# Keys and values of both full branches as one Strassen block of seven products, with the sums of h formed earlier

## Chip, cores, metric

One core of one Trainium2 chip. The metric is the device time of one launch in microseconds (us), the median of several executions.

## What is computed

One layer of a decoder, 512 tokens by 2048 channels, fp32. The part that matters here is the input projection and what it feeds:

```python
h = rms_norm(x, norm_g[l])
proj = h @ w_in[l]
q, kv, g_logits, z_a, uv, z_b, merge_logits = jnp.split(proj, SPLIT_IDX, axis=-1)
k_c, v_c, k_s, v_s, k_w, v_w = [t.reshape(b, s, A_KV_GROUPS, HEAD_DIM)
                                for t in jnp.split(kv, 6, axis=-1)]
# compress(): hid = silu(blocks of 32 rows of k_c (v_c) plus positions, times w1), then times w2
o_a = nsa_attention(q, k_c, v_c, k_s, v_s, k_w, v_w, g_logits, ...) * jax.nn.silu(z_a)
```

Three branches of attention (compressed `_c`, selected `_s`, window `_w`) have keys and values of 256 columns each: 4 groups of 64. The 48 gate columns `g_logits` weigh the branches. The rest of the layer (gated MLP branch, merge, output projection, per-layer embedding, final norm) is not touched.

## The kernel before

Every fp32 product is made of three fp32r matmuls. A matrix is split into a high part (a cast on ACT, `high`, L158) and a low part (a subtraction on DVE, `low`, L164), and hi·hi, hi·lo and lo·hi are summed in PSUM. The activation h lies in SBUF in both parts (`act_h`, `act_l`); weights are streamed.

The products of h are jobs in a list, and a generator (`gemm`) issues them in order. `fill(n)` takes n units of it (a unit is three matmuls in a T job), `finish(name)` runs it to the end of a job. So the order on PE is written by hand: whatever the main program issues between two calls stands there in each engine's queue, and each engine runs its queue in order. Three kinds of job are met here:

- T: 128 columns of weights stationary, all 512 tokens moving: 16 k × 3 = 48 matmuls of 512 columns; the result lies transposed (columns on partitions). q0 to q7, z0 to z7, kc0 and kc1 (keys, compressed branch), vc0 and vc1 (its values), k00 to k11 (keys of the other two branches) are T jobs.
- N: 128 tokens stationary, up to 512 columns of weights moving; 16 k × 4 token tiles × 3 = 192 matmuls. vs and vw are N jobs of 256 and of 304 columns (the last 48 of vw are the gates).
- S: a block of 2·c columns and all tokens is done with seven products of quarter blocks in place of eight (Strassen in Winograd's form); the products are named by digits and their order is "15", "63", "7", "24". It needs sums of quarters of the weights (`sum_to`, on DVE) and four sums of quarters of h. Job u, much later, is the first of the S jobs that use the sums of h.

A job takes its weights in subs: 12 matmuls with one piece of hi and lo. `split_to` keeps the splits two subs ahead of PE. Loads are issued on SP (`load_next`), three raw buffers; streamed hi and lo have a few buffers each. At each sub `pop()` takes an item off `background` and off `slow` at set rates; `flush()` runs what was put off in `deferred`, such as the second half of a split.

The order is kc0 kc1 vc0 vc1 k00 k01 k10 k11 vs vw q0 q1 z0 and so on. Compression runs beside k: token rows in `tok`, `ps_hid` (L1186), a chain of small DVE and ACT operations (L1190 to L1208, a tanh in it), then `ps_kc` and `ps_vc` (L1211, L1215). The four sums of h are made in four chunks (`h_chunk`, L483, 12 DVE operations each) beside k, vs, vw and q, through `h_stage` tiles and DMAs into DRAM (L511).

## Time and profile before

| | |
|---|---|
| median of 3 executions | 1515.46 us (1515.12 to 1515.68) |
| profiled execution | 1515.4 us, of it span 1513.7 us |
| mean granted TensorE clock | 0.998 |
| PE busy | 1502.4 us (99%) |
| DVE, ACT, POOL busy | 1216.4, 857.5, 377.6 us |

The span is what the profile covers, from the first instruction to the last. Rows of matmuls give the latency of one; they overlap, so the time that one takes of PE is the distance from its start to the next one's. Names are those of tiles (buffer numbers left out), L-numbers are lines of the kernel before.

### The profile page before, as it was taken

To read this page: it belongs to the slowest core of one execution; us is meant where nothing else is said; L and a number is where in the kernel's file an instruction comes from. 1 tells how busy PE (TensorE), PEld (TensorE's weight loads), DVE (VectorE), ACT (ScalarE), POOL (GpSimd) and SP (SyncE) were. 2 spreads that over 40 slices of the span, in tenths; PEclk is the share of its full clock that TensorE was granted. 3 is DMA by queue.
4 is the path that set the end of the run, shared out by engine and by line. 5 is a ranking of instruction groups with operands and counts; after the bars stand their busy time and mean duration, and the time that the engine had idled before them with its cause. 6 is when DMAs were issued, how large, how long until landed. Compare 5 with 4: busy or idle time off the path is not lost.

```text
span 1513.7 us, 20632 instructions
## 1 busy us (share of the span) xinstructions
PE 1502.4 (99%) x7269; PEld 1261.9 (83%) x7269; DVE 1216.4 (80%) x1871; ACT 857.5 (57%) x1492; POOL 377.6 (25%) x595
## 2 busy tenths in 40 slices
PE   9999999999999999999999999999999999999997
PEld 8889988888888888888888888888888888888886
DVE  7557768899997888978888878797877985687877
ACT  6544456777675565555655555555556555444556
POOL 1311223323433232333333424421110002100000
PEclk9999999999999999999999999999999999999999
DMA  9676778778776895978686968896797869945555
GB/s 329 188 167 199 236 158 213 180 158 240 168 189 214 254 294 142 293 153 283 145 266 180 271 179 262 235 305 250 271 322 245 246 188 332 312 169 183 181 208 192
DMA packets 187351, 340.54 MB, mean 225 GB/s; under 512 B 12520, under 2 KB 84848, under 8 KB 184048
## 3 DMA queue, kind: packets, MB, share of 16 engines
q0 software_dynamic: 67216, 168.42, 40.6%
q1 hardware_dynamic: 119888, 170.55, 35.0%
q8 instruction: 57, 0.93, 0.2%
q14 instruction: 46, 0.38, 0.1%
q10 hardware_dynamic: 144, 0.26, 0.0%
HBM read 278.88 MB, written 109.58 MB: 257 GB/s over the span
## 4 chain that ended last, share of the span: by engine, by line
PE 95%; DVE 3%; ACT 1%; DMA 0%; issue 0%; DVEq 0%; ACTq 0%
PE ps_m L399 7%; PE ps_m L401 7%; PE ps_m L400 7%; PE ps_wo L400 3%; PE ps_wo L401 3%; PE ps_wo L399 3%; PE ps_t L1323 2%; PE ps_za L427 2%; PE ps_za L425 2%; PE ps_za L426 2%; PE ps_u L399 2%; PE ps_ub L400 2%; PE ps_u L400 2%; PE ps_ub L401 2%; PE ps_pg L401 2%; PE ps_pg L399 2%
## 5 line engine op out<-in xcount | busy, mean ns | idle before, releaser
L164 DVE TENSOR_TENSOR ls<-b,hs 128x1024 fp32r<-128x1024 f32 x218 | 266.4, 1223 | 108.4 <-ACT hs L158 107.2
L158 ACT CAST hs<-b 128x1024 fp32r<-128x1024 f32 x218 | 229.3, 1053 | 200.1 <-PE ps_m L401 46.0
L158 ACT CAST hs<-raw 128x1024 fp32r<-128x1024 f32 x114 | 120.0, 1055 | 116.9 <-issue 34.1
L164 DVE TENSOR_TENSOR ls<-raw,hs 128x1024 fp32r<-128x1024 f32 x114 | 139.3, 1222 | 39.5 <-ACT hs L158 39.3
L164 DVE TENSOR_TENSOR lo<-raw,hi 128x512 fp32r<-128x512 f32 (+1 forms) x152 | 100.6, 668 | 36.4 <-issue 9.9
L158 ACT CAST hi<-raw 128x512 fp32r<-128x512 f32 (+1 forms) x152 | 89.8, 601 | 60.5 <-PE ps_pg L440 10.8
L399 PE MATMUL ps_m<-hs,act_h 128*128 128x512 f32 x256 | 100.1, 391 | 0.0
L401 PE MATMUL ps_m<-hs,act_l 128*128 128x512 f32 x256 | 99.7, 389 | 0.0
L400 PE MATMUL ps_m<-ls,act_h 128*128 128x512 f32 x256 | 99.6, 389 | 0.0
L282 DVE TENSOR_TENSOR b<-raw,b 128x1024 f32<-128x1024 f32 x72 | 87.7, 1218 | 2.6 <-DMA raw<-in_w_in_dram 2.6
L282 DVE TENSOR_TENSOR b<-b,b 128x1024 f32<-128x1024 f32 x72 | 87.7, 1218 | 0.0
L158 ACT CAST pth<-ps_t 128x512 fp32r<-128x512 f32 (+1 forms) x88 | 47.7, 543 | 47.5 <-PE ps_t L1323 46.9
L1282 ACT ACTIVATE prob<-prob,st 128x512 f32<-128x512 f32 (+3 forms) x128 | 70.7, 556 | 4.3 <-DVE st L1273 3.9
L358 POOL COPY pad_r<-pad_r 128x1 f32<-128x1 f32 x42 | 32.1, 764 | 136.4 <-ACT pad_r L357 136.4
L164 DVE TENSOR_TENSOR ptl<-ps_t,pth 128x512 fp32r<-128x512 f32 (+1 forms) x88 | 55.7, 637 | 10.7 <-ACT pth L158 10.0
L1273 DVE CUSTOM_DVE_ANT_0 prob<-ps_s,b 128x512 f32<-128x512 f32 (+3 forms) x128 | 56.2, 486 | 2.5 <-PE ps_s L1264 2.1
L401 PEld LDWEIGHTS ps_m<-hs,act_l 128*128 128x128 f32 x256 | 48.0, 188 | 10.1
L400 PEld LDWEIGHTS ps_m<-ls,act_h 128*128 128x128 f32 x256 | 48.1, 188 | 9.9
L399 PEld LDWEIGHTS ps_m<-hs,act_h 128*128 128x128 f32 x256 | 48.1, 188 | 9.8
L425 PE MATMUL ps_za<-act_h,hi 128*128 128x512 f32 x128 | 53.5, 418 | 0.0
L1298 DVE TENSOR_SCALAR prob<-prob,st,gates 128x512 f32<-128x512 f32 (+3 forms) x128 | 51.5, 455 | 1.8
L425 PE MATMUL ps_q<-act_h,hi 128*128 128x512 f32 x128 | 52.0, 407 | 0.0
(705 smaller groups left out, 4557.4 us busy)
## 6 DMA issues: line engine op xcount, KB each, us to landing
raw<-in_w_in_dram SPq DMA_DIRECT2D x112, 512.0 KB, 5.2
b<-in_w_in_dram SPq DMA_DIRECT2D x56, 512.0 KB, 6.5
o<-in_w_out_dram POOLq DMA_DIRECT2D x48, 512.0 KB, 8.0
t<-in_w_up_b_dram POOLq DMA_DIRECT2D x24, 512.0 KB, 8.1
raw<-in_w_ple_gate_dram SPq DMA_DIRECT2D x24, 512.0 KB, 3.7
b<-o SPq DMA_DIRECT2D x18, 512.0 KB, 6.3
o<-o POOLq DMA_DIRECT2D x16, 512.0 KB, 5.1
act_l<-gate POOLq DMA_DIRECT2D x8, 1024.0 KB, 13.0
```

The costliest lines, as they stand in the source:

```text
L158: nc.scalar.copy(hi, src)
L164: nc.vector.tensor_tensor(out=lo, in0=src, in1=hi.bitcast(F32), op=ALU.subtract)
L282: nc.vector.tensor_tensor(out=b[o], in0=b[x], in1=b[y], op=ALU.subtract)
L358: nc.gpsimd.tensor_copy(steps[:, 16 + i:17 + i], steps[:, i:i + 1])
L399: nc.tensor.matmul(o, ah, wh, start=st, stop=False, skip_group_check=go)
L400: nc.tensor.matmul(o, ah, wl, start=False, stop=False, skip_group_check=go)
L401: nc.tensor.matmul(o, al, wh, start=False, stop=sp, skip_group_check=go)
L425: nc.tensor.matmul(ps, hi[:, j], ah, start=st, stop=False)
L426: nc.tensor.matmul(ps, hi[:, j], al, start=False, stop=False)
L1273: nc.vector.tensor_tensor_reduce(out=pt[:, j * n:j * n + n], in0=o[:, j], in1=b0[:, 512 - n:], scale=-SLOPE[h], scalar=3.0e38, op0=ALU.add ...
L1282: nc.scalar.activation(sl, sl, AF.Exp, bias=st[:, 0, j, hh:hh + 1], scale=-1.0, accum_out=st[:, 1, j, hh:hh + 1])
L1298: nc.vector.tensor_scalar(out=sl, in0=sl, scalar1=st[:, 1, j, hh:hh + 1], scalar2=gates[:, i, gate:gate + 1], op0=ALU.mult, op1=ALU.mult)
```

## The change

- The four k jobs, vs and vw become one S job `kv` of 1024 columns: K and V of the window branch and K and V of the selected branch, seven products of 48 matmuls of 512 columns. Products 1 and 5 are split in halves of 512 columns on the streamed hi and lo tiles (`narrow`), the others on wider tiles `hs` and `ls`; one quarter of the weights is read twice. K comes out with tokens on partitions, so `turn_k` transposes it on PE (16 transposes of 128×128, `ps_kt`), and DMAs on POOL copy half of the rows across partitions.
- vc0 and vc1 become an N job `vcg` of 304 columns: 256 of the compressed values and the 48 gates, by two DMAs per load. It stands between kc0 and kc1. ACT copies its rows out, and `turn_vc` transposes them back (8 transposes, `ps_vct`).
- The order is kc0 vcg kc1 q0 kv q1 z0 and on.
- The sums of h are needed by kv, so they are made from vcg on, at 0.7 items per sub instead of 0.5, in place (`ob_h`, `ob_l`, `vt`) for three of them. They are still stored to DRAM for job u. The fourth goes through streamed tiles `h_hi`, `h_lo` to DRAM, and is read back into `ob_h` before product 7.
- The splits of w1 (compression) are put into `background` ahead of the chunks of h, at vcg's first subs; they stood behind vc0.
- The mask `b0` is made at the start of attention, and no longer ahead of the compression.

```diff
-    def h_chunk(c, pool):
+    def h_chunk(c, temps, homes):
...
+        def put(p, src):
+            o = homes[p][:, k1]
+            parts_later(o[:, :, lo_t], o[:, :, hi_t], src, lambda: nc.gpsimd.dma_start(hsum_dram[p][:, k1], o))
+
+        def put_7(src):
+            o = [stream.tile([P, 2, 256], F32R, tag=tag, name="h_" + tag, bufs=n) for tag, n in (("hi", 4), ("lo", 3))]
+
+            def store():
+                for sl, part in zip((lo_t, hi_t), o):
+                    nc.gpsimd.dma_start(h3_dram[:, k1, sl], part)
+            parts_later(*o, src, store)
...
+    def final_kv(t, c, o, src):
+        if o is None:
+            if t == 2:
+                kv_rows["last"] = quad["pool"].tile([P, 2, S], F32, tag="hs", name="c21", bufs=3)
+            o = kv_rows["last"][:, t - 2]
+            nc.scalar.copy(o, src)
+        b = 0 if c else 1
+        kv_rows[b, t] = o
+        split(vt[:, b, t, :, 0:HD], vt[:, b, t, :, HD:], o[:, 256:].rearrange("p (g d) -> p g d", g=GROUPS), later=True)
+        if t == 3 or b and t == 1:
+            deferred.append(partial(turn_k, b, t // 2))
+            if not b:
+                later(partial(turn_k, b, 0))
+
+    def turn_k(b, hf):
+        ps = bank("o", "ps_kt")
+        for a in range(2):
+            for t in range(2):
+                nc.tensor.transpose(ps[:, (2 * a + t) * P:(2 * a + t + 1) * P],
+                                    kv_rows[b, 2 * hf + t][:, a * P:a * P + P], ident)
...
+            for o in (ob_h, ob_l):
+                for e in range(2):
+                    g = slice(kk(b, e), 8, 4)
+                    nc.gpsimd.dma_start(o[rows[1 - e], g, sl], o[rows[e], g, sl])
+        deferred.append(lows)
...
+    def evac_vcg(ps):
+        for t in range(TT):
+            nc.scalar.copy(vc_rows["t"][:, t], ps[t][:, :256])
+            nc.scalar.activation(gates[:, t], ps[t][:, 256:304], AF.Tanh, scale=0.5)
+            nc.vector.tensor_scalar(out=gates[:, t], in0=gates[:, t], scalar1=1.0, scalar2=0.5,
+                                    op0=ALU.add, op1=ALU.mult)
+
+    def turn_vc(a):
+        ps = bank("s", "ps_vct")
+        for t in range(TT):
+            nc.tensor.transpose(ps[:, t * P:t * P + P], vc_rows["t"][:, t, a * P:a * P + P], ident)
+        evac_c(1, a)(ps)
...
-    for a in range(2):
-        add_job(Job(f"vc{a}", "T", w_in, C_KV + 256 + 128 * a, 128, KT, h_act, evac_c(1, a)))
...
-    add_job(Job("vs", "N", w_in, C_KV + 768, 256, KT, h_act, evac_v(0), vs_b))
-    add_job(Job("vw", "N", w_in, C_KV + 1280, 304, KT, h_act, evac_v(1), vw_b))
+    kc_job(0)
+    add_job(Job("vcg", "N", w_in, ((slice(0, 256), C_KV + 256), (slice(256, 304), C_G)), 304, KT, h_act, evac_vcg,
+                ("o", "o", "t", "t")))
+    kc_job(1)
...
+    def evac_kv(p, ps):
+        quad_kv(p, ps)
+        if p == "5":
+            for c in range(4):
+                nc.gpsimd.dma_start(ob_h[:, 2 * c:2 * c + 2], h3_dram[:, 2 * c:2 * c + 2])
+
+    q_job(0)
+    add_job(Job("kv", "S", w_in, C_KV + 1024, 512, KT, lambda p, k, t: kv_act(p, k, t), evac_kv, ("s", "g", "t"),
+                c2=C_KV + 512, narrow="15"))
...
+        state["pops"] = 0.7
+        finish("vcg")
+        fill(2)
+        turn_vc(0)
+        fill(2)
+        turn_vc(1)
+        fill(1)
...
-    with tc.tile_pool(name="hsum", bufs=1) as hsum:
-        state["rate"] = 0
-        for c in range(4):
-            background.extend(h_chunk(c, hsum))
-        state["pops"] = 0.5
-        finish("q1")
...
+    finish("kv")
+    assert not background
+    fill(8)
...
+    ph_x.close()
+    finish("q1")
```

What the change moves in three queues, row by row. First ACT, at the end of the N job that holds the gates. Before, this job is vw: its rows are split straight into `vt`, each followed by a gate's tanh (L571), and q0's weights stand behind.

```order
L158 CAST hi<-raw 128x512 x2
L158 CAST vt<-ps_vw_1589 128x4x64
L571 ACTIVATE gates<-ps_vw_1589 128x48
L158 CAST vt<-ps_vw_1590 128x4x64
L571 ACTIVATE gates<-ps_vw_1590 128x48
L158 CAST vt<-ps_vw_1591 128x4x64
L571 ACTIVATE gates<-ps_vw_1591 128x48
L158 CAST vt<-ps_vw_1592 128x4x64
L571 ACTIVATE gates<-ps_vw_1592 128x48
L158 CAST hi<-raw 128x512 x4
```

Now ACT at the end of vcg; `ob_l` and `h_hi` are highs of chunk 1 of h, `o_584` a scratch tile that holds vc's rows and the temporaries of h.

```order
L158 CAST ob_l<-o_584 128x2x256
L158 CAST h_hi<-o_584 128x512
L615 COPY o_584<-ps_vcg_625 128x256
L616 ACT_TABLE_LOAD
L616 ACTIVATE gates<-ps_vcg_625 128x48
L615 COPY o_584<-ps_vcg_626 128x256
L616 ACTIVATE gates<-ps_vcg_626 128x48
L615 COPY o_584<-ps_vcg_627 128x256
L616 ACTIVATE gates<-ps_vcg_627 128x48
L615 COPY o_584<-ps_vcg_628 128x256
L616 ACTIVATE gates<-ps_vcg_628 128x48
L158 CAST hi<-raw 128x512
```

The table load, which stood ahead of the tanh of the compression (L1205), moved to the first tanh of the gates, and two highs of h stand directly ahead of the copies.

PE at the same place, from vcg's last matmul on (line numbers of the kernel after; `ps_vct` are the transposes of vc's rows). Before, PE has no transposes of results here: vc0 and vc1 are T jobs.

```order
L461 MATMUL ps_vcg_628<-hi,act_l_95 128x304
L446 MATMUL ps_kc_1003<-act_h_88,hi 128x512
L447 MATMUL ps_kc_1003<-act_l_89,hi 128x512
L448 MATMUL ps_kc_1003<-act_h_88,lo 128x512
L446 MATMUL ps_kc_1003<-act_h_88,hi 128x512
L447 MATMUL ps_kc_1003<-act_l_89,hi 128x512
L448 MATMUL ps_kc_1003<-act_h_88,lo 128x512
L623 MATMUL ps_vct<-ident,o_584 128x128 x4
L446 MATMUL ps_kc_1003<-act_h_88,hi 128x512
```

Two units of kc1 stand between the two; the transposes read what the four copies write.

DVE around the compression's chain. Before (L1199 to L1208), the weights of a k job are split ahead of it.

```order
L642 TENSOR_TENSOR tok<-ps_vc_805,tok 64x8x32 x4
L164 TENSOR_TENSOR lo<-raw,hi 128x512 x4
L1199 TENSOR_TENSOR o_580<-ps_hid_947,o_580 64x136
L1199 TENSOR_TENSOR o_580<-ps_hid_948,o_580 64x136
L1200 TENSOR_TENSOR o_580<-o_580 128x136
L1202 TENSOR_TENSOR hid_c<-o_580 128x1
L1203 SCALAR_TENSOR_TENSOR o_580<-o_580,hid_c 128x128
L1206 SCALAR_TENSOR_TENSOR o_580<-o_580 128x128
L1208 TENSOR_SCALAR o_580<-o_580 128x4x32 x4
L558 TENSOR_TENSOR ob_l<-ps_k_899,ob_h 64x512 x2
```

After (L1277 to L1286 are the same operations); L301 is a sum of weights for product 5, L504 are sums of h, `b_1052` is kv's quarter of weights.

```order
L301 TENSOR_TENSOR b_1052<-b_1052,raw 128x1024
L164 TENSOR_TENSOR lo<-raw,hi 128x512 x2
L504 TENSOR_TENSOR o_584<-act_h_94,o_584 128x512
L504 TENSOR_TENSOR o_584<-o_584,act_l_95 128x512
L164 TENSOR_TENSOR ob_l<-o_584,ob_l 128x2x256
L164 TENSOR_TENSOR h_lo<-o_584,h_hi 128x512
L164 TENSOR_TENSOR lo<-b_1052,hi 128x512 x2
L1277 TENSOR_TENSOR o_584<-ps_hid_1200,o_584 64x136
L1277 TENSOR_TENSOR o_584<-ps_hid_1201,o_584 64x136
L1278 TENSOR_TENSOR o_584<-o_584 128x136
L1280 TENSOR_TENSOR hid_c<-o_584 128x1
L1281 SCALAR_TENSOR_TENSOR o_584<-o_584,hid_c 128x128
```

The chain now stands behind kv's first lows, a sum of kv's weights and operations of chunk 2 of h.

PE at the end of kv (`ps_kt` are the transposes of K's rows, `c_1932` a row tile that ACT copies out of `ps_kv`):

```order
L420 MATMUL ps_kv_1313<-hs,act_h_94 128x512
L421 MATMUL ps_kv_1313<-ls,act_h_94 128x512
L422 MATMUL ps_kv_1313<-hs,act_l_95 128x512
L592 MATMUL ps_kt<-ident,c_1932 128x128 x4
L592 MATMUL ps_kt<-ident,keep_1491 128x128
...
L446 MATMUL ps_q_1950<-act_h_88,hi 128x512
```

Before, vw's last matmul is followed by q0's first at once:

```order
L438 MATMUL ps_vw_1592<-hi,act_h_94 128x304
L439 MATMUL ps_vw_1592<-lo,act_h_94 128x304
L440 MATMUL ps_vw_1592<-hi,act_l_95 128x304
L425 MATMUL ps_q_1935<-act_h_88,hi 128x512
L426 MATMUL ps_q_1935<-act_l_89,hi 128x512
```

So between the N or S job's end and the q job that follows, transposes of the last rows now stand.

## The prediction

> **What bounds the kernel now.** I read the page's totals first, then the chain, then the stretch that the change rewrites, cut into windows by job. On the page:

> ```profile
> span 1513.7 us, 20632 instructions
> PE 1502.4 (99%) x7269; PEld 1261.9 (83%) x7269; DVE 1216.4 (80%) x1871; ACT 857.5 (57%) x1492; POOL 377.6 (25%) x595
> PE 95%; DVE 3%; ACT 1%; DMA 0%; issue 0%; DVEq 0%; ACTq 0%
> ```

> TensorE is the bound: 99% busy, 95% of the chain. A microsecond of matmul removed is a microsecond gained, and a microsecond that PE waits is one lost. The windows, one row per stage (busy us and instructions of each engine), run from the end of kc0 to the start of z0; before them and behind them the two programs issue the same matmuls.

> ```profile
> 47.00:57.95 10.95, 10.95 (x50) 9.05 (x49) 4.37 (x8) 4.14 (x10) 8.29 (x19) 1.00 0.73 216
> 57.95:79.88 21.93, 21.93 (x98) 18.08 (x97) 12.36 (x28) 10.45 (x26) 5.55 (x12) 1.00 0.64 185
> 79.88:128.53 48.65, 48.65 (x235) 40.87 (x234) 30.94 (x56) 23.34 (x47) 7.14 (x11) 1.00 0.77 184
> 128.53:151.57 23.04, 23.04 (x194) 23.03 (x192) 17.28 (x29) 9.78 (x20) 2.66 (x5) 1.00 0.63 191
> 151.57:178.03 26.46, 26.46 (x194) 26.46 (x193) 22.80 (x42) 12.82 (x28) 4.26 (x8) 1.00 0.75 221
> 178.03:199.81 21.78, 21.78 (x98) 18.02 (x97) 8.67 (x17) 7.55 (x17) 6.22 (x16) 1.00 0.90 255
> ```

> The rows are kc1; vc0 and vc1; the four k jobs with the compression; vs; vw; q0 and q1. PE is full in all, at granted clock 1.00. A matmul's row lasts longer than its share (they are pipelined), so I count from start to start: 96 matmuls of 512 columns in q's 21.78 us are 0.227 us each, 192 of 256 columns in vs's 23.04 us 0.120, 192 of 304 in vw's 26.46 us 0.138. The k row holds 192×0.227 = 43.6 and 5.1 of compression. DVE has 6 to 18 us to spare in every long row but vw's, where 3.7 are left.

> **The gross gain.** Behind kc0 the new stretch holds vcg (192 matmuls of 304 columns, vw's form, 26.5), kc1 (11.0), q0 and q1 (21.8), compression (5.1), kv (7 products × 48 = 336 matmuls of 512 columns, 336×0.227 = 76.2), and 24 transposes of 128×128. For those the nearest rows are eight of the same shape, and the matmul behind them:

> ```profile
> 26.27 1.03 PE L1034 MATMUL ps_x<-ident,xt 128*128 128x128 f32 x8
> 27.06 0.47 PE L438 MATMUL ps_pl<-hi,ob_h 128*128 128x512 f32 x1
> ```

> Eight take 0.79, so 24 take 2.4. Together 26.5 + 11.0 + 21.8 + 5.1 + 76.2 + 2.4 = 143.0 against 152.8 before: 9.8 us less, if PE never waits. So the question is how much of 9.8 us comes back as waits. DVE must do the sums of h (four chunks of 12 operations), vc's lows and kv's lows and sums in less PE time, and several PE instructions now stand close behind results of ACT and DVE. The prices:

> ```profile
> L164 DVE TENSOR_TENSOR lo<-raw,hi 128x512 fp32r<-128x512 f32 x46 | 31.1, 689 | 21.2 <-issue 6.5 <-PE ps_k L427 4.9 <-PE ps_q L427 4.1
> L483 DVE TENSOR_TENSOR h<-h,act_l 128x512 f32<-128x512 f32 x8 | 5.5, 692 | 0.3
> L282 DVE TENSOR_TENSOR b<-raw,b 128x1024 f32<-128x1024 f32 x72 | 87.7, 1218 | 2.6 <-DMA raw<-in_w_in_dram 2.6
> 135.30 0.69 DVE L483 TENSOR_TENSOR h<-h_b,act_h 128x512 f32<-128x512 f32 x1
> 136.02 0.69 DVE L483 TENSOR_TENSOR h<-h,act_l 128x512 f32<-128x512 f32 x1
> 136.63 0.68 DVE L164 TENSOR_TENSOR lo<-raw,hi 128x512 fp32r<-128x512 f32 x1
> L158 ACT CAST hi<-raw 128x512 fp32r<-128x512 f32 x48 | 28.9, 621 | 27.6 <-PE ps_q L426 8.4 <-PE ps_k L426 6.0 <-PE ps_vc L426 4.9
> L158 ACT CAST vt<-ps_vw 128x256 fp32r<-128x256 f32 x4 | 1.5, 368 | 0.0
> L571 ACT ACTIVATE gates<-ps_vw 128x48 f32<-128x48 f32 x4 | 0.8, 210 | 2.0 <-DVE vt L164 2.0
> ```

> A DVE operation of 512 elements is listed at 0.69; the next one starts 0.72 later if it needs the result (135.30 to 136.02), 0.61 if not (136.02 to 136.63). A chunk of h is thus 12×0.61 to 12×0.69, 7.3 to 8.3.

> **The waits, in PE's order.**

> (a) Start of vcg. DVE's rows there:

> ```profile
> 48.91 1.73 DVE L642 TENSOR_TENSOR tok<-ps_kc,tok 64x256 fp32r<-64x256 f32 x4 [2.84 <-ACT tok L638]
> 50.68 1.29 DVE L164 TENSOR_TENSOR lo<-raw,hi 128x512 fp32r<-128x512 f32 x2
> 45.00 0.56 POOL L1129 IOTA b<- 128x512 f32 x1 [11.21 <-DVE act_l L166]
> 45.64 0.90 POOL L1130 TENSOR_SCALAR_AFFINE_SELECT b<-b 128x512 f32<-128x512 f32 x1
> 50.08 1.21 POOL L1156 DMA_DIRECT2D o<-in_cmp_w_k_dram  x1
> o<-in_cmp_w_k_dram POOLq DMA_DIRECT2D x1, 512.0 KB, 5.1
> ```

> kc0's four token lows hold DVE until 50.6. Before, the job there has subs of 12×0.227 = 2.7 us, so two subs of lead cover it; vcg's subs last 12×0.138 = 1.7, and the third comes due near 50.4 with its low still to run: 0.65 lost (0 to 0.7). Two subs later the low stands behind the first split of the compression's weights w1. That split stood behind vc0, long after its data; now it stands in vcg's second sub, on ACT and DVE both. Its DMA leaves POOL at 48.6 (50.08 less the two operations on b, 1.5, which move to the attention's start) and lands 5.1 later, at 53.7, while PE needs the fifth sub's low near 54.5 and the split's own two operations and the low come first: nothing if the landing holds, 2.5 if the queue of weight loads delays it. I take 0.5.

> (b) End of vcg. Only six matmuls of kc1 (1.4 us) stand between vcg's last one and the transposes of vc (ps_vct), which read ACT's copies of all four banks. Interleaved with these copies are the gates' tanh, and ahead of the first tanh the table load that now is in the compression's chain:

> ```profile
> 93.28 0.18 ACT L357 COPY pad_r<-eps_t 128x1 f32<-128x1 f32 x1
> 93.48 1.28 ACT L1205 ACT_TABLE_LOAD   x1
> 94.77 0.31 ACT L1205 ACTIVATE o<-o 128x128 f32<-128x128 f32 x1
> ```

> Four copies (4×0.37), three tanh (3×0.21) and the load (1.28) are 3.4 us of ACT before the last copy is there, so PE waits 3.4 − 1.4 = 2.0 at least. That needs ACT free at vcg's end. It isn't: the highs of chunk 1's second and third sum (ob_l, h_hi, 0.62 each) stand ahead and wait for DVE's two subtractions, which stand behind a low whose buffer is released by vcg's last sub. Low, subtractions and highs overlap into about 1.9 more. I take 3.9; upper end 4.3. DVE loses the same time, because the gates' scaling stands next in its queue and waits for the tanh.

> The row shows a load of 1.28 us, 0.02 behind the copy before it. [...]

> (c) Compression. Its DVE chain before:

> ```profile
> 91.18 0.69 DVE L164 TENSOR_TENSOR lo<-raw,hi 128x512 fp32r<-128x512 f32 x1 [4.91 <-PE ps_k L427]
> 91.90 0.29 DVE L1199 TENSOR_TENSOR o<-ps_hid,o 64x136 f32<-64x136 f32 x1
> ...
> 95.12 0.29 DVE L1206 SCALAR_TENSOR_TENSOR o<-o 128x128 f32<-128x128 f32 x1 [1.16 <-ACT o L1205]
> 95.44 0.63 DVE L1208 TENSOR_SCALAR o<-o 128x128 f32<-128x128 f32 x4
> 98.00 0.38 PE L1211 MATMUL ps_kc<-o 128*128 128x128 f32 x2
> ```

> From 91.90 to 96.07 it takes 4.2, or 2.9 without the table load. Before, PE has 6.1 us of k matmuls between the start of the chain and ps_kc, and no wait. Now two lows of kv's second sub stand directly ahead of the chain (the order of DVE shows it), and the second of them needs a buffer that kv's first sub frees as it ends. PE has then one unit of three matmuls (0.7) before ps_kc. So PE waits 0.69 + 2.9 − 0.7 = 2.9, and some 0.1 for signals: 3.0. Lower end 1.6 (the chain's operations, 2.3, without their waits, less the unit), upper 4.0 (with one more operation ahead). Directly behind it, kv's next bank is held by q0, whose two lows stand behind the chain: 0 to 1.0; I take 0.5.

> (d) kv's first two products. Eight subs are 8×2.7 = 21.8 us of PE. DVE owes in them sixteen lows, four sums of weights, the last chunk of h, the chain and q0's lows: 16×0.61 + 4×1.22 + 7.8 + 2.9 + 1.4 = 26.7. With the 3.0 of (c) there is 24.8 of room, so 1.9 would be late if DVE had no lead; the last sub of product 5 also needs the last chunk's sums written. With the h temporaries' waits I reach 3.2 as the upper end; 0 if DVE enters with a lead of two subs. I take 1.6, and 0.3 (0 to 1.0) for the same backlog in kc1 and q0.

> (e) End of kv. PE's order has the transposes of the last K rows (ps_kt) directly behind kv's last matmul; they wait for two ACT operations of 512 columns (2×0.62) less what overlaps: 1.0 (0.6 to 1.2). Before, vw's banks were read by ACT while q0's matmuls ran.

> At nothing: kv's narrow DMAs and the h sums written to and read from DRAM, because each issue costs POOL half a microsecond and a sum is needed again no sooner than one product (10.9 us) later:

> ```profile
> 128.56 0.53 POOL L511 DMA_DIRECT2D hsum<-h_stage  x1 [8.18 <-DVE h_stage L164]
> raw<-in_w_in_dram SPq DMA_DIRECT2D x112, 512.0 KB, 5.2
> ```

> The weight loads on SP (5.2 to land) have three buffers, and kv takes five quarters of weights in 76 us. If that cover fails, a late load costs at most its landing, 5.2. The DMAs that copy K rows across partitions, and b's two operations, have q1 and z0 (14.8 us) before the first compressed scores: 8×0.53 + 1.5 + a landing of 5.2 is 10.9, so 0 to 1.0.

> **Sum.** Waits: 0.65 + 0.5 + 3.9 + 3.0 + 0.5 + 1.6 + 0.3 + 1.0 = 11.45. With all lower ends 2.0 + 1.6 + 0.6 = 4.2, with all upper ends 0.7 + 2.5 + 4.3 + 4.0 + 1.0 + 3.2 + 1.0 + 1.2 + 1.0 = 18.9. Net −9.8 + 11.45 = +1.65. The profiled execution took 1515.4 us (span 1513.7), within 0.1 of the median 1515.46, so 1517.1. The ends are 1515.4 − 5.6 = 1509.8 and 1515.4 + 9.1 = 1524.5.

> **Rivals.**
> 1. DVE becomes the bound (slower). From vcg to the end of product 5 PE has 26.5 + 11.0 + 10.9 + 5.1 + 0.8 + 21.8 = 76.1 us of own work. DVE has 16 lows of 304 columns (0.47), 76 operations of 512 elements (48 of h, 24 lows, 4 of w1; 0.69), 16 token lows (0.42), four sums (1.22), and 6.5 of chain, positions, gates and q0's lows: 7.5 + 52.4 + 6.7 + 4.9 + 6.5 = 78.0. My forecast grants it 76.1 + 10.45 (all waits but (e)) = 86.5, so it decides from 8.5 us of idle time of DVE on; each further one is one on the end. Its idle in the gates is 3.9. The row of lows above shows 21.2 us of idle ahead of 46, 0.46 each; 24 of them would add 11.0, if all of it were waits for buffers: 78.0 + 3.9 + 11.0 = 92.9, 6.4 over. With half of them it is 0.9 over. The middle, 3.6, gives 1520.7. For it speaks that two of my large waits are such buffers already; against it that before, DVE idled there because it was ahead.
> 2. DVE and ACT run ahead (faster). If chunk 1's highs are done when vcg ends, (b) is 2.0; if the lows come early enough, (c) is 1.6, (d) and (a) vanish and (e) is 0.6 to 1.0. Waits of 4.6: 1510.2. For it speaks the spare DVE time in the k and q rows; against it that buffers, not DVE's speed, hold the low in (b) and in (c).
> 3. A gap slows PE afterwards. (b) and (c) are waits of 3 to 4 us of a PE that had none in the rows above; if behind each the granted clock (1.00 in all six) stood at half for as long as the gap, matmuls would lose half of 3.9 + 3.0: 1517.1 + 3.4 = 1520.5. No row shows such a fall. [...] No gap of this trace can test it.

> **How the numbers follow.** 0.2% (3 us) is about what a measurement of this kernel can tell from no change. My forecast is that the waits eat the gain: 1517.1, own range 1512.4 to 1518.5, chance 0.38. Rival 1 has 0.28 and rival 3 0.06: slower 0.34. Rival 2 has 0.28: faster. Cases of both signs hold most of the chance, so the range goes out to the bounds of the sum: from 1509.0 (0.8 below the lower bound, which keeps (b) and (c) in any case) to 1522.5 (2.0 short of the upper one, which needs every wait at its worst; about 1 in 10 is left out at either end).

> **What would show it.** Right: vw's, vs's and vc's stages gone, kv 76 us of matmuls at 0.227; PE idle 2 to 4 us before the first ps_vct, released by ACT's copy; 2 to 4 before ps_kc, released by DVE's scaling; 1 before the last ps_kt, released by ACT. Wrong: PE's busy time in the stretch not 143 but more; less than 4 us of idle on PE; a wait for a DMA in kv; a granted clock under 1.00 behind a gap.

## The result and the profile after

The changed kernel takes 1535.78 us (median of 4, 1533.57 to 1538.05) against 1515.29: ratio 1.0135, 95% interval 1.0118 to 1.0153. It is 20.5 us slower. I had forecast 1517.1 with a range to 1522.5, so the forecast was wrong.

The profile's page has these lines where before's had PE at 99% and a clock of 9 tenths throughout (the third line is the granted clock in 40 slices of 38 us):

```profile
span 1535.4 us, 20496 instructions
PE 1505.3 (98%) x7149; PEld 1255.2 (82%) x7149; DVE 1247.4 (81%) x1897; ACT 870.7 (57%) x1509; POOL 390.2 (25%) x620
PEclk9979999999999999999999999999999999999999
```

Fewer matmuls are issued (7149 against 7269), and one slice, 77 to 115 us, has a mean clock of 0.7. The same stretch as in the prediction, from vcg's first matmul to z0, by windows (vcg; kc1; q0 with the hidden products; kv with the end of the compression; last transposes and q1; the column ahead of the last two is the granted clock, the next the share of the DMA engines):

```profile
47.17:75.52 28.35, 26.99 (x193) 26.49 (x192) 19.58 (x38) 13.43 (x37) 17.65 (x33) 1.00 0.87 258
75.52:97.13 21.61, 15.39 (x59) 11.70 (x58) 13.18 (x32) 10.17 (x26) 6.97 (x10) 0.76 1.15 277
97.13:118.31 21.18, 17.58 (x82) 14.51 (x81) 13.60 (x22) 8.42 (x21) 5.35 (x11) 0.84 0.99 305
118.31:206.95 88.64, 82.84 (x356) 65.85 (x354) 72.76 (x97) 42.97 (x67) 15.12 (x25) 0.98 0.71 193
206.95:219.63 12.68, 12.09 (x57) 9.97 (x58) 7.58 (x16) 7.12 (x17) 8.61 (x17) 1.00 0.73 169
```

Together 172.5 us where before had 152.8, so 19.7 of the 21.7 us between the two spans are lost here (the profiled execution took 1537.06 us, 1.3 above the median). kc1 takes 21.6 for 11 us of matmuls. The waits of PE (line, releaser: total us, times, longest):

```profile
PE ps_vct L623 <- issue: 4.9, 1, 4.9
PE ps_q L448 <- DVE lo L164: 3.6, 1, 3.6
PE ps_kc L1289 <- issue: 2.5, 1, 2.5
PE ps_kv L421 <- DVE lo L164: 2.0, 2, 1.3
PE ps_vcg L460 <- DVE lo L164: 1.4, 2, 0.8
PE ps_vct L623 <- ACT o L615: 1.3, 1, 1.3
PE ps_kv L420 <- DVE b L166: 1.0, 1, 1.0
PE ps_m L421 <- DVE ls L164: 1.0, 2, 0.7
PE ps_kt L592 <- ACT c L579: 0.6, 1, 0.6
```

These are the places that I had named, (a) to (e), and one that I had at 0.3: q0, 3.6. What stands ahead of the two longest is seen on ACT and DVE (start, duration, idle time ahead and its releaser):

```profile
79.76 0.62 ACT L158 CAST hi<-raw 128x512 fp32r<-128x512 f32 x1 [2.27 <-DMA h_d<-h_hi]
98.84 0.62 ACT L158 CAST hi<-raw 128x512 fp32r<-128x512 f32 x1 [3.40 <-DMA h_d<-h_hi]
100.61 0.69 DVE L164 TENSOR_TENSOR lo<-raw,hi 128x512 fp32r<-128x512 f32 x1 [4.23 <-DMA h_d<-h_lo]
```

A split of weights waits for a DMA that *stores* a sum of h, because the sum sits in a slot of the same ring of buffers. Ahead of ps_vct stands such a split in ACT's queue, then two highs of h and the copies; the store's 2.27 us are thus a part of PE's 4.93. And the matmuls behind the wait:

```profile
76.68 0.40 PE L448 MATMUL ps_kc<-act_h,lo 128*128 128x512 f32 x1
82.00 0.45 PE L623 MATMUL ps_vct<-ident,o 128*128 128x128 f32 x1 [4.93 <-issue]
83.74 1.24 PE L623 MATMUL ps_vct<-ident,o 128*128 128x128 f32 x3 [1.29 <-ACT o L615]
84.63 0.77 PE L446 MATMUL ps_kc<-act_h,hi 128*128 128x512 f32 x1
85.20 0.63 PE L447 MATMUL ps_kc<-act_l,hi 128*128 128x512 f32 x1
85.63 0.63 PE L448 MATMUL ps_kc<-act_h,lo 128*128 128x512 f32 x1
```

From 84.63 on a matmul lasts 0.63 in place of 0.39, and the next starts after 0.43 in place of 0.23: half clock (the granted clock reads 0.50 from 80 to 88 us).

### The profile page after: what moved, and what is told of

Read it like the earlier page. It is cut to its first block, busy times and chain, and to the rows that moved or that the text cites. A ratio compares the mean times of both kernels' runs of the same rounds, so it can differ in the third digit from the quotient of the medians.

```text
span 1535.4 us, 20496 instructions
## 1 busy us (share of the span) xinstructions
PE 1505.3 (98%) x7149; PEld 1255.2 (82%) x7149; DVE 1247.4 (81%) x1897; ACT 870.7 (57%) x1509; POOL 390.2 (25%) x620
## 5 line engine op out<-in xcount | busy, mean ns | idle before, releaser
L164 DVE TENSOR_TENSOR ls<-b,hs 128x1024 fp32r<-128x1024 f32 x224 | 273.9, 1223 | 110.7 <-ACT hs L158 109.1
L158 ACT CAST hs<-b 128x1024 fp32r<-128x1024 f32 x224 | 235.3, 1052 | 208.6 <-PE ps_m L422 51.0
L158 ACT CAST hs<-raw 128x1024 fp32r<-128x1024 f32 x126 | 132.8, 1054 | 122.5 <-issue 28.8
L164 DVE TENSOR_TENSOR ls<-raw,hs 128x1024 fp32r<-128x1024 f32 x126 | 154.1, 1223 | 41.1 <-ACT hs L158 40.8
L164 DVE TENSOR_TENSOR lo<-raw,hi 128x512 fp32r<-128x512 f32 (+1 forms) x128 | 83.8, 662 | 26.4 <-ACT hi L158 8.7
L158 ACT CAST hi<-raw 128x512 fp32r<-128x512 f32 (+1 forms) x128 | 74.8, 597 | 47.2 <-PE ps_pg L461 10.4
L301 DVE TENSOR_TENSOR b<-raw,b 128x1024 f32<-128x1024 f32 x78 | 95.1, 1219 | 4.9 <-DMA raw<-in_w_in_dram 4.8
L301 DVE TENSOR_TENSOR b<-b,b 128x1024 f32<-128x1024 f32 x72 | 87.8, 1219 | 0.0
L158 ACT CAST pth<-ps_t 128x512 fp32r<-128x512 f32 (+1 forms) x88 | 47.7, 544 | 48.1 <-PE ps_t L1405 47.5
L164 DVE TENSOR_TENSOR ptl<-ps_t,pth 128x512 fp32r<-128x512 f32 (+1 forms) x88 | 55.6, 636 | 10.2 <-ACT pth L158 9.5
L448 PE MATMUL ps_q<-act_h,lo 128*128 128x512 f32 x128 | 51.4, 402 | 3.6 <-DVE lo L164 3.6
## 6 DMA issues: line engine op xcount, KB each, us to landing
raw<-in_w_in_dram SPq DMA_DIRECT2D x112, 512.0 KB, 5.5
b<-in_w_in_dram SPq DMA_DIRECT2D x59, 512.0 KB, 6.7
o<-in_w_out_dram POOLq DMA_DIRECT2D x48, 512.0 KB, 8.3
t<-in_w_up_b_dram POOLq DMA_DIRECT2D x24, 512.0 KB, 8.5
raw<-in_w_ple_gate_dram SPq DMA_DIRECT2D x24, 512.0 KB, 3.8
b<-o SPq DMA_DIRECT2D x18, 512.0 KB, 6.2
o<-o POOLq DMA_DIRECT2D x16, 512.0 KB, 5.2
```

What stands on the lines that cost most here:

```text
L158: nc.scalar.copy(hi, src)
L164: nc.vector.tensor_tensor(out=lo, in0=src, in1=hi.bitcast(F32), op=ALU.subtract)
L301: nc.vector.tensor_tensor(out=b[o], in0=b[x], in1=b[y], op=ALU.subtract)
L448: nc.tensor.matmul(ps, lo[:, j], ah, start=False, stop=sp)
```

## The experiments

Every kernel is timed against the kernel before on the same chip. Unless said otherwise an edit is made to the kernel after. I had two new theories beside my forecast's waits: **the crowd** (DMAs are slow in this stretch and hold ring slots and weights back) and **the clock** (behind a wait PE runs at half clock for a while).

**1. No crowd.** The background loads (adding DMAs for sums of other weights, `t<-in_w_up_b`, 512 KB each) are issued at 0.7 per sub. vcg's subs last 1.7 us and not 2.7, so the unchanged rate per sub is a higher rate per microsecond (from 60 to 75.5 us five are issued, where before had two), and the stores of h come in the same stretch. First they were held back into kv, then behind kv:

```diff
-        state.update(rate=0.7, step=0)
+        state.update(rate=0.0, step=0)
...
-    state["rate"] = 0        # first kernel only, with rate 0 again behind kv
+    state["rate"] = 0.65
...
-    state.update(rate=1.2, step=None)   # second kernel only
+    state.update(rate=1.5, step=None)
```

> The kernel after, with the background loads (adding DMAs for sums of other weights, 512 KB each, on POOL's queue, 0.7 per sub) held back until the compression is done, and issued at 0.65 per sub during kv. Theory of the crowded queue (vcg's subs last 1.7 us in place of 2.7, so the same rate per sub puts these DMAs closer, and the stores of h land after 10 us in place of 4): the stores land in about 5 us, the waits ahead of ps_vct and in q0 shrink as without the ring, about 8 us less, near 1528, unless kv's own weight loads are delayed. Rival (the stores are slow by themselves): landings of about 10 us stay, 1536.

> The kernel after, with none of the background loads (512 KB adding DMAs on POOL's queue) from vcg to the end of kv; they come later, at 1.5 per sub in place of 1.2. Theory of the crowded queue: as with the loads held back to kv (the wait ahead of ps_vct 2.3, none of weight in q0), but without the 2.4 us wait for a weight load that they made in kv: the stretch from vcg to z0 some 5 us shorter than there, near 1528. What is left then are my forecast's waits for ACT and DVE: about 4.5 at ps_vct, 4 at ps_kc, 2.5 in kv's first products, 0.8 at its end. Rival (the wait in kv has its own cause): 1532 again.

Measured 1533.60 (ratio 1.0118, 1.0102 to 1.0133) and 1528.09 (1.0084, 1.0067 to 1.0101). The DMAs issued from 70 to 104 us, first after, then the first kernel (KB each, median us from issue to landing):

```profile
h_d<-h_hi POOLq DMA_DIRECT2D x2, 256.0 KB, 10.2
raw<-in_w_in_dram SPq DMA_DIRECT2D x4, 512.0 KB, 11.9
```

```profile
raw<-in_w_in_dram SPq DMA_DIRECT2D x5, 512.0 KB, 4.3
h_d<-h_hi POOLq DMA_DIRECT2D x2, 256.0 KB, 3.6
```

The landings fall to a third, as the theory has it. In the first kernel kv then waits for its own weights (2.4 us at one low); in the second nothing of that is left, and PE's waits are

```profile
PE ps_kc L1289 <- issue: 2.6, 1, 2.6
PE ps_vct L623 <- issue: 2.1, 1, 2.1
PE ps_kv L421 <- DVE lo L164: 2.0, 2, 1.3
PE ps_vct L623 <- ACT o L615: 1.4, 1, 1.4
```

with none at q0. The crowd costs 7.7 us (1535.8 to 1528.1), and what stays is my forecast's list and two spells of half clock.

**2. Own slots for h_hi and h_lo**, the crowd left in:

```diff
-            o = [stream.tile([P, 2, 256], F32R, tag=tag, name="h_" + tag, bufs=n) for tag, n in (("hi", 4), ("lo", 3))]
+            o = [cmp.tile([P, 2, 256], F32R, tag="h_" + tag, name="h_" + tag, bufs=1) for tag in ("hi", "lo")]   # chunks 0 to 2
```

> The kernel after, with h_hi and h_lo of the first three chunks on tiles of their own in place of slots of the streamed hi and lo rings. Theory of the ring (a slot that holds a sum of h is free only when its store into DRAM has landed, 10 to 11 us later, and the weights' splits queue behind it on ACT and DVE): the wait ahead of ps_vct falls from 5.1 to about 3 us, the 3.8 us wait in q0 goes, and with it q0's stretch at half clock (2.5): about 8 us less, near 1528. Rival (those splits are late because ACT's and DVE's queues are full): the same two waits, 1536.

Measured 1530.64 (1.0098, 1.0083 to 1.0114). The wait in q0 is gone, but ps_vct's grew from 4.9 to 6.8:

```profile
81.62 0.62 ACT L158 CAST hi<-raw 128x512 fp32r<-128x512 f32 x1 [4.49 <-DMA raw<-in_w_in_dram]
```

The same split now waits for its weights, which land after 15.2 us. So the slot is one way in which the crowded queues reach PE, and the late loads another; expectation right for q0, wrong for ps_vct.

**3. The table load ahead of vcg.**

```diff
         state["pops"] = 0.7
+        nc.scalar.activation(warm, eps_t, AF.Tanh)
         finish("vcg")
```

> The kernel after, with a tanh of one column ahead of vcg's last subs' evacuation, at vcg's start, so that the table load is done there. My forecast's step (the load of 1.28 us stands between the copies that ps_vct needs): the second wait at ps_vct (1.3 to 1.6 us, between its first transpose and the others) goes; 1.3 us less, 2 if the half clock ends sooner: 1534. Rival (the load is covered): 1536, or 1 more for the token lows that it delays at vcg's start.

Measured 1537.11 (1.0140, 1.0125 to 1.0155): no gain. The second wait at ps_vct went as expected, but q0's wait for the same DMAs rose from 3.6 to 5.4 us. What was gained ahead of the late DMA was lost again in the wait for it.

**4. Spare matmuls in the waits**, to keep PE busy.

```diff
+        for _ in range(20):     # ahead of ps_vct; 16 ahead of q0, 8 ahead of ps_kc
+            nc.tensor.matmul(ps, act_h(0, slice(0, P)), act_h(0), start=True, stop=True)
```

> The kernel after, with idle PE time filled: 20 spare matmuls of 512 columns ahead of the first ps_vct, 16 ahead of q0's first matmul and 8 ahead of ps_kc, each into a bank that the next real matmul starts afresh. Nothing else moves, and 44 matmuls (10 us of PE) are added. Theory of the clock (a PE that waits some 3 us falls to half clock and stays there for 5 to 8 us): the granted clock stays at 1.00 from 75 to 110 us, the matmuls of kc1 and q0 come every 0.227 us, about 8 us less, near 1528. Rival (the clock's fall costs nothing of its own; the waits for ACT, DVE and DMA set the time): 1536, or up to 2 more where the spare matmuls run over.

Measured 1536.21 (1.0132, 1.0115 to 1.0149): the same as after, so the forecast of 8 us failed. In q0, where the spares filled the wait, the clock stayed at 1.00 and z0 began 2.8 us earlier than in after (216.9 against 219.6). At ps_vct they ran out 1.6 us before the first copy was there, and the clock fell all the same, only later. Some 1.8 us of that were lost again behind z0, 1.0 of them in a wait for lows of weights in job vn that after doesn't have; why there, was not tried. As a test of the clock this one is inconclusive, so the clock was measured by itself.

**5. One wait in the kernel before**, between vs and vw, which nothing else depends on:

```diff
+        nc.tensor.transpose(gb[:, :P], hold, ident)
+        for _ in range(12):     # 30 in the other
+            nc.gpsimd.memset(hold, 0.0)
+        nc.tensor.transpose(gb[:, P:2 * P], hold, ident)
         finish("q1")
```

> The kernel before, with one wait put into PE's queue between vs and vw: a transpose, twelve small fills on POOL of the tile that it read, and a second transpose that needs the last fill. Nothing else depends on it, so the time is the wait plus what the clock adds. The wait is estimated at about 2 us. Theory of the clock (it falls only behind a wait of more than some 3 us): granted clock stays 1.00, +2 us, 1517.5. Rival (any wait of 2 us already halves it): 1520.

> As the kernel before with one wait between vs and vw, but of thirty fills, estimated at about 5 us. Theory of the clock: the granted clock falls to 0.5 in the wait and stays there for some 4 to 7 us of matmuls behind it; the time grows by the wait and 2 to 3.5 us more: 1522.5 to 1524. Rival (the clock's fall is a reading of the profile and costs nothing): the wait alone, 1520.4.

Measured 1521.59 (+6.1; ratio 1.0041, 1.0026 to 1.0056) and 1525.37 (+9.8; 1.0066, 1.0051 to 1.0081). The waits came out longer than estimated, 3.4 and 8.1 us from start to start:

```profile
151.38 0.27 PE L1228 MATMUL ps_gap<-ident,hold 128*128 128x128 f32 x1
154.86 0.48 PE L1231 MATMUL ps_gap<-ident,hold 128*128 128x128 f32 x1 [3.21 <-POOL hold L1230]
```

```profile
150.96 0.27 PE L1228 MATMUL ps_gap<-ident,hold 128*128 128x128 f32 x1
159.17 0.47 PE L1231 MATMUL ps_gap<-ident,hold 128*128 128x128 f32 x1 [7.94 <-POOL hold L1230]
```

The windows where the clock falls and where it returns, the short wait first:

```profile
152.00:154.00 2.00, 0.00 (x0) 0.00 (x0) 0.80 (x3) 0.30 (x1) 1.60 (x8) 0.93 0.00 0
160.00:162.00 2.00, 2.00 (x14) 2.00 (x14) 0.99 (x3) 1.07 (x2) 0.00 (x0) 0.87 0.49 148
```

```profile
154.00:156.00 2.00, 0.00 (x0) 0.00 (x0) 0.00 (x0) 0.00 (x0) 1.56 (x8) 0.82 0.00 0
162.00:164.00 2.00, 2.00 (x16) 2.00 (x16) 1.52 (x3) 0.45 (x1) 0.00 (x0) 0.97 0.02 3
```

A window of 2 us with a mean of 0.93 holds 0.28 us at half clock, so the short wait's half clock runs from 153.72 to 160.52, the long one's (0.82, 0.97) from 155.28 to 162.12: 6.8 us both times. Of the first, 5.7 fall on matmuls, which lose half of it: 3.4 + 2.8 = 6.2, measured 6.1. Of the second, 2.9 do: 8.1 + 1.5 = 9.6, measured 9.8. The clock costs time of its own (for the long wait the times alone don't show it, since the interval, 7.7 to 12.3 us, includes 8.1; for the short one they do), and a longer wait may pay less for it, since more of the spell passes in the wait. My expectation that the cost grows with the wait was wrong; as the short wait came out at 3.4 us, whether one of 2 us is free was not tested here. The fall came 2.2 us after PE's last matmul in one and 4.2 in the other, so not at a fixed time behind it.

**6. The transposes of vc later**, with no crowd and the table early:

```diff
-        fill(2)
+        fill(8)
         turn_vc(0)
```

> As the kernel without the crowd, and the tanh table loaded at vcg's start and eight units of kc1 (in place of two) ahead of the first ps_vct. Theory of the place (the transposes stand too close behind ACT's copies): the waits at ps_vct (4.5 in all) and the half clock behind them (1.2) go, 1.5 of them come back as a wait for the token lows ahead of ps_hid or in q0: near 1523. Rival (ACT and DVE owe the work anyway, and the wait moves on to kc1's weights): no more than 2 us less.

Measured 1523.40 (1.0054, 1.0039 to 1.0069). No wait at ps_vct is left, nor a fall of the clock there; 1.4 us came back as a wait for a low in q0 and 0.4 as one in kc1. The two edits were not tried apart, but the last of the four copies and the first transposes tell their shares:

```profile
79.49 0.43 ACT L615 COPY o<-ps_vcg 128x256 f32<-128x256 f32 x1
80.68 0.60 PE L623 MATMUL ps_vct<-ident,o 128*128 128x128 f32 x4
```

The copies are done 0.8 us before PE gets there. With the load of 1.28 us still between them they would have come some 0.5 us late (an estimate), so nearly all of the 4.7 us is the later place.

**7. Own slots again, and the last transposes of K a sub later**, on top of that kernel (for K: `deferred.append(lambda: deferred.append(partial(turn_k, b, t // 2)))`).

> The last kernel (no crowd, table early, transposes of vc eight units later) with h_hi and h_lo of the first three chunks on tiles of their own, and the last transposes of K deferred by one sub. Theory (the wait ahead of ps_kc is for a slot of the streamed lo ring that h_lo holds; the last ps_kt stands too close to its copies): ps_kc's wait 2.7 goes to about 1.3, half of the clock's fall behind it goes, the last wait at ps_kt 0.8 goes: near 1520. Rival (DVE's total work in the stretch is what binds, so what goes there returns in kv): 1523 as before.

Measured 1522.53 (1.0045, 1.0030 to 1.0060), 0.9 below experiment 6 and not clear of it: the intervals overlap. ps_kc's wait fell from 2.6 to 1.2 as expected. But the clock fell there nevertheless, and the wait at ps_kt stayed at 0.6, since only the other half of these transposes moved. The fall came at 109.72, about half way through a second wait of 1.0, so a wait of 1.2, ten short products and some 0.5 us more were enough for the clock.

**8. Ten spare matmuls ahead of that ps_kc**, the clock's second test:

```diff
         b = bank("o", "ps_kc")
+        for _ in range(10):
+            nc.tensor.matmul(b, act_h(0, slice(0, P)), act_h(0), start=True, stop=True)
```

> The kernel with own slots for h_hi and h_lo (no crowd, table early, transposes of vc later), with ten spare matmuls of 512 columns (2.3 us of PE) ahead of ps_kc, where PE waits 1.3 us and, right behind ps_vc, 1.3 again. Theory of the clock: the fall to half clock from 110 to 117 us, which I put at about 2.5 us there, doesn't come, and though work is added the time falls by 1.5 to 3 us: 1520. Rival (the clock's fall is not what costs there; PE waits for DVE's lows anyway): 1522.5 as before, or up to 1 more.

The windows of the kernel without the spares, then with them:

```profile
110.00:112.00 2.00, 1.63 (x4) 1.37 (x5) 1.97 (x4) 0.00 (x0) 0.00 (x0) 0.50 0.71 262
112.00:114.00 2.00, 2.00 (x6) 1.52 (x6) 1.89 (x4) 0.62 (x1) 0.00 (x0) 0.50 0.16 28
```

```profile
110.00:112.00 2.00, 1.79 (x8) 1.51 (x9) 1.97 (x4) 0.57 (x1) 0.00 (x0) 1.00 0.74 270
112.00:114.00 2.00, 2.00 (x11) 1.64 (x10) 2.00 (x4) 0.94 (x3) 0.00 (x0) 1.00 0.13 18
```

Eleven matmuls fit where six did. 2.3 us of work were added, the stretch from vcg to z0 is 2.3 us shorter (155.2 against 157.5), and the median is 1521.01 (1.0043, 1.0029 to 1.0057). That is 1.5 below, but single runs of the two kernels overlap and their ratios to before (1.0043 and 1.0045) are alike, so the trace shows it and the times only point to it.

**9. Additions of h on POOL, and a new order**, on top of experiment 7:

```diff
-                add(w[n], act_h(k1, t), act_l(k1, t))
+                nc.gpsimd.tensor_tensor(out=w[n], in0=x, in1=y, op=ALU.add)
```

> As that one, with the two first additions of each chunk of h on POOL in place of DVE (8 operations, some 5 us of DVE; an addition of this shape is 1.1 us on POOL in the trace of before). Theory of DVE as the bound in this stretch: the waits for lows in q0 (1.5) and in kv's first products (2.8) shrink by about 3 together: near 1517. Rival (those waits are for order and slots, or POOL and DVE hold each other up): no less, or 1 to 2 more.

Measured 1526.89 (1.0074, 1.0059 to 1.0089), 4.4 worse; the rival was right, and by more than it said. DVE, then POOL:

```profile
71.29 4.25 DVE L164 TENSOR_TENSOR lo<-raw,hi 128x304 fp32r<-128x304 f32 x2
84.38 3.11 DVE L504 TENSOR_TENSOR o<-o,act_l 128x512 f32<-128x512 f32 x1
```

```profile
72.06 2.54 POOL L547 TENSOR_TENSOR o<-act_h,act_l 128x512 f32<-128x512 f32 x2
84.39 2.54 POOL L547 TENSOR_TENSOR o<-act_h,act_l 128x512 f32<-128x512 f32 x2
```

Two lows that take 0.85 at 60.69 in the same trace take 4.25 here, and an addition of 0.69 takes 3.11, each until less than 1 us behind the end of POOL's pair. PE's waits for lows grew by 1.1 us in vcg and 1.6 in q0.

The last kernel put two empty items ahead of w1's splits, 0.8 items per sub and the compression two units earlier (`fill(7)` for `fill(9)`), all on top of POOL's additions:

> As the one with POOL's additions, with two empty items ahead of the splits of w1 (so that their DMA has landed), 0.8 items per sub in place of 0.7, and the compression's products two units earlier in q0, which puts its chain on DVE ahead of kv's second lows. Theory (every wait of the stretch is one of place): a's second wait (0.9) goes, ps_kc's and the bank's wait behind it fall to 1 to 2 together, the clock no longer falls: 1512 to 1515, at or below the kernel before. Rival (DVE binds): within 1 of the one before.

Measured 1528.92 (1.0092, 1.0075 to 1.0109). (a)'s second wait went, but PE then waited 3.5 us ahead of ps_hid for the lows of the tokens, and 2.1 in q0, and the clock fell twice. Since it was built on the additions on POOL, it says nothing on the order without them.

## Why the prediction was wrong

The stretch from vcg to z0, in us of the profiled execution. Waits are measured from start to start, less the matmul's own share.

| | forecast | after | no crowd |
|---|---|---|---|
| PE's own work | 143.0 | 145.1 | 145 |
| (a) vcg | 1.15 | 1.7 | 1.4 |
| (b) ps_vct | 3.9 | 7.3 | 4.5 |
| kc1 and q0 | 0.3 | 3.8 | 0 |
| (c) ps_kc and the bank behind it | 3.5 | 4.1 | 4.1 |
| (d) kv's first products | 1.6 | 2.8 | 2.8 |
| (e) last ps_kt | 1.0 | 0.8 | 0.8 |
| half clock | 0 | about 7 | about 5 |
| sum | 154.5 | 172.5 | 163.4 |

The half clock of after has three spells. The windows in which each begins and ends, read as above:

```profile
78.00:80.00 2.00, 0.00 (x0) 0.00 (x0) 1.34 (x3) 0.24 (x1) 0.00 (x0) 0.81 1.28 299
88.00:90.00 2.00, 2.00 (x8) 1.56 (x7) 0.99 (x3) 1.93 (x6) 0.00 (x0) 0.63 1.14 202
98.00:100.00 2.00, 0.00 (x0) 0.00 (x0) 0.00 (x0) 1.16 (x3) 0.34 (x2) 0.93 1.05 183
106.00:108.00 2.00, 2.00 (x8) 1.57 (x8) 1.97 (x4) 0.45 (x1) 0.00 (x0) 0.86 1.06 352
126.00:128.00 2.00, 1.22 (x4) 0.99 (x5) 1.97 (x3) 0.23 (x2) 1.68 (x3) 0.76 0.65 240
130.00:132.00 2.00, 2.00 (x9) 1.57 (x9) 1.08 (x3) 0.98 (x3) 0.41 (x2) 0.89 1.19 173
```

They run from 79.24 to 89.48, 99.72 to 106.56 and 127.04 to 130.44: 10.2, 6.8 and 3.4 us, all multiples of 3.4. Matmuls fill 84.6 to 89.5, 101.4 to 106.6 and the third; half of these is 6.7, and some tenths are for the transposes. In the last column the half clock is what the rest leaves; its two spells, counted as above, give 4.4.

The spells begin 20.48 and 27.32 us apart, six and eight times 3.41. In the second kernel of experiment 1 they begin 37.52 apart, eleven times 3.41, and in the two of experiment 9 20.48 and 10.24, six and three times (all within 0.04). Lay this grid of 3.41 us over PE's gaps in this stretch of after and of the kernels of experiments 1 (the second), 6, 7 and 9, and around the two waits of experiment 5, and what went ahead of a fall shows: each of the 11 steps of the grid at full clock in which PE had 2.05 us or more without work ended in half clock (2.3 and 2.1 us ahead of the first two spells above, 2.05 in the first kernel of experiment 9). Six steps with 1.9 to 2.03 us didn't, and of all those with less than 2.05 only two did, with 1.6 us (experiment 9) and 2.0 (experiment 7) and the compression's ten short products in them. These sums of gaps are estimates from the traces, from start to start with 0.227 us for a matmul of 512 columns, 0.11 for one of the short products.

Right were the gross gain (the matmuls that go and come) up to 2.1 us, the places of the waits, and without the crowd their sizes: 13.6 against 11.45. (d) was 2.8 where I halved 3.2 on the hope that DVE gains a lead. The matmuls of kv's last five products come every 0.231 to 0.235 us and not every 0.227, which is about 1.5 of the 2.1. The clock is 1.00 there, and job m's matmuls of the same form come every 0.227 in the same trace; the cause was not tried.

The step that failed is "At nothing: kv's narrow DMAs and the h sums written to and read from DRAM". I counted what the issue costs POOL and when a sum is needed again, and took landings from rows where the queue had room. I did not ask who waits for the *slot* from which a sum is stored, and I did not count the background loads, whose rate per sub the diff leaves alone while it shortens the sub. "If that cover fails, a late load costs at most its landing, 5.2" was wrong too: the landings themselves went to 10 to 12. With the background loads out of the stretch the kernel takes 7.7 us less. The stretch itself was 18.0 us longer than forecast. Of these 9.1 go with the loads: 6.9 of waits and some 2 of half clock. Of the 8.9 that stay some 4.5 are half clock, 2.2 waits and 2 PE's own work.

The second failure is rival 3, the clock. I gave it 0.06 because no row of before showed a fall, though before has no wait to show one. Its price of 3.4 in all is about 7 in after, because three spells came and their length is a multiple of 3.4 us, not that of the wait. The waits of 3.4 and 8.1 us both brought a fall, but the limit of some 3 us in the expectation of experiment 5 is too high for these traces: 2.1 us without work inside one step of 3.41 were enough.

Rival 1 (DVE becomes the bound) had the sign, not the cause: DVE is 73 of 88.6 us busy from kv's start to its end, but only 61 and 64% busy in the windows of kc1 and q0, where the time went. In kv's first two products it is fuller, 22.5 of 24.5 us from 121 to 145.5; whether its work is what binds in (d) stays open, since experiment 9 also made DVE slower. Rival 2 (waits hidden) is out.

About 2 us are lost behind z0, 1.3 of them where job m waits for lows of weights; this differs from kernel to kernel and stays open. No version beat the kernel before: the best, experiment 8, is at 1521.0, where (a), (d), (e) and q0 still hold some 7 us of waits.

## What to carry to other kernels

Where a change shortens the steps to which background transfers are tied, work out their rate per microsecond anew, and ask of every store which ring its source sits in and who takes the next slot. In a kernel whose PE was never idle, a wait can cost more than its length: here a wait of 3.4 us cost 6.1. Waits that can't be removed should be filled, or kept so short and far apart that no 3.4 us hold 2 us of them (the 2 us are an estimate from the gaps above; the second was not tried by itself). A wait can only be judged with the one behind it: the early table load took 1.3 us off one wait, and the next one grew by 1.8.
